# Sixteen attention heads on one core: the order of the steps inside a head

## The chip, the cores and the metric

The kernel is one program on 1 core of one Trainium2 chip. Time is device microseconds of one execution, the median of several runs. The profile is one execution taken by the hardware profiler; its span runs from the first to the last instruction of the program.

## What is computed

One inference step of a two-layer encoder trunk for a prompt (one sequence of 512 frames) and a sample group (8 sequences of 16 new frames, each with 512 cached frames). Layer 0 is a recurrent layer. The residual stream after it gives one shared K and V, and layer 1 is stick-breaking attention with 16 heads of 128 features. The change lies in layer 1 alone; cut to it:

```python
def sb_block(q, q_pos, k, v):
    z = jnp.einsum('bqhd,bshd->bhqs', q, k).astype(jnp.float32) * (HEAD_DIM ** -0.5)
    mask = jnp.arange(k.shape[1])[None, :] < q_pos[:, None]
    log_keep = jnp.where(mask, jax.nn.log_sigmoid(-z), 0.0)
    log_after = lax.cumsum(log_keep, axis=3, reverse=True) - log_keep
    attn = jnp.where(mask, jnp.exp(jax.nn.log_sigmoid(z) + log_after), 0.0)
    o = jnp.einsum('bhqs,bshd->bqhd', attn, v.astype(jnp.float32))

def stick_breaking_mixer(hn, k_all, v_all, w_in, w_out):
    q, zg = jnp.split(hn @ w_in, 2, axis=-1)
    o = stick_breaking(q.reshape(B, T, N_HEADS, HEAD_DIM), k_all, v_all)
    return (o.reshape(B, T, D_ATT) * jax.nn.silu(zg)) @ w_out
```

For each head there are a score matrix, an elementwise function with a running sum from the right, and a sum of value rows weighted by the result. The prompt's queries see the prompt's own keys; the sample's 16 queries of each sequence see its 512 cached keys and its 16 new ones.

## The kernel before

The heads run one after the other (`heads`, L1847). While the attention of head h runs, the query and gate projection of head h+1 is computed beside it, in slices: `query` (L1506) is a generator, and each `next` of it (a step "q") records 12 to 36 matmuls of 128x128 weights against 320 tokens, into the tiles `psh`. A head has 180 of these. In the last head, "q" advances the output projection instead (tiles `acc`, weights `w_out_b`). The float32 operands are split into a high and a low part on ScalarE and VectorE (L1367/L1368 for the weights), and each product takes three matmuls (L108 to L110).

The steps of a head are written as a string of letters, one for the usual head (`ORDER`, L1845) and one for the last (`LAST`, L1844):

- P, `prompt_scores` (L1796): scores of four query rows of blocks, 12 matmuls of 128 weight columns into `z3`, `z2` and `z1`, and 8 matmuls of 32 weight columns for the sample's new keys into the rest of `z1` (L1809). Each goes through `sticks` (L1628): ScalarE abs, exp, ln (L1637 to L1639), VectorE max, scan, subtract (L1642, L1645, L1648), ScalarE exp (L1649), a mask on GpSimd (L1653).
- S0, S1, `sample_scores(g)` (L1723): four matmuls (L1727) of 32 weight columns each against 512 cached keys, one for each of four sequences, into four partition groups of `zc`; then `sticks`. S0 issues the load of the second half's cached keys `ck`.
- V0, V1, `prompt_turn` (L1813): the prompt's attention is transposed on TensorE (`pa`, L1713), copied to `ath` by ScalarE (L1719), and its remainder to `atl` by VectorE (L1720).
- T0, T1, `sample_turn(g)` (L1746): issues the loads of the cached values `cv`, transposes the sample's attention (`pas`, four, and `pan`, one), copied out to `at` and `an`.
- O, `prompt_out` (L1821): 12 matmuls into `po`.
- M0, M1, `sample_out(g)` (L1759): the sum over the values, all with 32 weight columns: four matmuls over the 16 new rows (L1763, operands `an` and `vn`) and 16 over cached rows (L1768, `at` and `cv`), into `pos`; copied out to `ob` by ScalarE (L1771). M0 issues the load of the second half's new values `vn`.
- C0, C1, `sample_close(g)` (L1773): `ob` transposed (`pot`, L1775), multiplied with the gate (L1778); in C1 the head's result is also split into `oh` and a remainder (L1790, L1791) and written to memory by two DMAs of GpSimd's queue (L1793, to `odh` and `odl`).
- L, U, N load the next head's keys, values and first cached keys on SyncE's queue; K and W split them. The raw keys `kr` use the same buffer as `oh`, so L's load waits for the write of `oh`.

An instruction that takes float32 operands as they are (L1727, L1763, L1768, L1809) goes through the array twice and stands twice in the trace: four instructions are eight records.

`pa`, `pas`, `pan`, `po`, `pos` and `pot` take turns in one ring of two PSUM banks (`bank`, L75). `ob`, `at`, `an`, `vn`, `ath`, `atl` and `oh` have one buffer each, `cv` and `ck` two, that is one half's worth. The tile framework's scheduler makes the order on each engine: it follows the written order, puts what can go now ahead of what it takes to be still waiting, and moves up what stands under a high priority (the weight splits, the copies of `psh`).

In the words below a *narrow* matmul is one of 32 weight columns (L1809, L1727, L1763, L1768), and a *narrow block* is a run of them with no other matmul between.

Of the kernel before, what the change touches and what calls it, by code (L numbers as in the profile page):

```python
# [19 lines left out]
P = 128  # L20
# [25 lines left out]
X12, X22, X11, S1, S2, S3, S4 = range(7)  # L46
# [4 lines left out]
class Trunk:  # L51
# [709 lines left out]
    S0 = 3 + TP  # L761
# [926 lines left out]
    def attention(self, h, ap, qkv, zs):  # L1688

        nc, I, O = self.nc, self.I, self.O  # L1690
# [43 lines left out]
        def new_values(g):  # L1734
            t = ap.tile([TS, 4, P], F32, tag="vn", name="vn", bufs=1)
            dma = (nc.gpsimd if g else nc.sync).dma_start
            rows = O["v"][TP + 64 * g : TP + 64 * g + 64, P * h : P * h + P]
            dma(t, rows.rearrange("(b t) d -> t b d", t=TS))
            return t
# [89 lines left out]
        o = zs  # L1829
        if h == NHEAD - 1:  # L1830
            o = self.outs.tile([P, 2, 3 * HALF], F32R, tag="ks1", name="o", bufs=1)[:, 0, :T].bitcast(F32)
        st = {"vn": new_values(0)}
        steps = {"P": prompt_scores, "O": prompt_out}
        for g in range(2):
            steps[f"V{g}"] = lambda g=g: prompt_turn(g)
            steps[f"T{g}"] = lambda g=g: sample_turn(g)
# [4 lines left out]


    STAY = (NHEAD - 2,)
    LAST = "P S0 q q q S1 V0 q V1 q Z T0 M0 O q C0 q T1 q M1 q C1 q"  # L1844
    ORDER = "P q q S0 L q q V0 V1 S1 T0 O U q M0 q T1 N K q C0 M1 W q C1"  # L1845

    def heads(self, count=NHEAD):  # L1847
        with self.pool("att") as ap:
            self.attention_consts(ap)
            self.qraw, self.qready = [None] * 4, {"wh": [], "wl": []}  # L1850
            for i in (0, 1, 3, 2):
                self.query_load(0, i)
            self.qplan = {"wh": self.product_plan(), "wl": self.plain_plan()}
            out = self.attention_begin()
            self.first_query(ap)
            keys, values = self.keys_load(0, ap), self.values_load(0, ap)
            self.ck = self.cached_keys(0, 0, ap)
            k, v = self.keys_split(ap, keys), self.values_split(ap, values)
            for h in range(count):
                qh, ql, qs, zs = self.q  # L1860
                steps = self.attention(h, ap, (qh, ql, qs, *k, *v), zs)
                more = h + 1 < count
                qn = self.query(h + 1, ap) if more else out
                for step in (self.ORDER if more else self.LAST).split():
                    if step == "q":
                        next(qn, 0)
                    elif step == "Z":
                        for j in range(2):
                            self.silu(ap, zs, j)
                    elif step in steps:  # L1870
                        steps[step]()
                    elif more and step == "L":
                        keys = self.keys_load(h + 1, ap)
                    elif more and step == "U":
                        values = self.values_load(h + 1, ap)
                    elif more and step == "N":
                        self.ck = self.cached_keys(h + 1, 0, ap)
                    elif more and step == "K":
                        k = self.keys_split(ap, keys)
                    elif more:  # L1880
                        v = self.values_split(ap, values)
        return out


# [111 lines left out]
def lay_out(r):  # L1996

    heads = lambda v, b: v.reshape(b, -1, NHEAD, P)
    y, k, v = r["y"], r["kT"].T, r["v"]
    state = r["state"].transpose(2, 1, 0).reshape(36, DR)  # L2000
    out = [y[:TP].reshape(1, TP, D), y[TP:].reshape(NB, TS, D), heads(k[:TP], 1), heads(v[:TP], 1), heads(k[TP:], NB),
           heads(v[TP:], NB), state[0:1].reshape(1, 1, DR), state[1:9].reshape(1, NB, DR),
           state[9:12].reshape(1, 1, 3, DR), state[12:].reshape(1, NB, 3, DR)]
    return tuple(np.ascontiguousarray(v) for v in out)
# [14 lines left out]
```

## Time and profile before

| | us |
|---|---|
| runs, median of 3 (lowest to highest) | 2859.81 (2859.26 to 2860.37) |
| span of the profiled execution | 2852.1 |
| what lies around the span | 7.7 |
| TensorE matmul busy in the span | 2785.0 (98%) |
| VectorE, ScalarE, GpSimd busy | 2034.8, 1666.2, 439.1 |
| the new keys' scores (L1809), of head 0 and of head 15, start at | 2020.9 and 2604.7 |

The profile gives the span alone of its execution; the runs' times are of other executions, and 7.7 us is the median less the span. The heads follow one another at 39 to 40 us, head 0 in less. In the views, a row of the timeline has the start, the duration, the engine and line, the operation, the tiles it writes and reads, its shape and how often it stands in a row, with the idle time before it and its releaser in brackets. Matmul ends are modelled: the steps from one start to the next tell how fast TensorE goes, and a matmul's duration is longer than its step.

### The profile page before, as it was taken

The numbers are of one execution on the slowest core, as the hardware profiler recorded it, in microseconds if no ns is written. First come the engines' busy times: TensorE is split into PE (matmuls) and PEld (weight loads), VectorE is DVE, ScalarE is ACT, GpSimd is POOL, SyncE is SP. The second block draws the span as 40 slices with busy tenths as digits, with TensorE's granted clock in tenths as the row PEclk, the third lists the DMA queues.
The fourth block names the chain that finished last, engine by engine and source line by source line (L and its number), as shares of the span: only waits on it lengthen the run. The fifth ranks groups of instructions, "written<-read, shape, count | busy, mean of one in ns | idle before, by whom it ended". The sixth has DMA issues, their size and how long they took to land.

```text
span 2852.1 us, 48054 instructions
## 1 busy us (share of the span) xinstructions
PE 2785.0 (98%) x18340; PEld 2459.3 (86%) x18340; DVE 2034.8 (71%) x3344; ACT 1666.2 (58%) x2846; POOL 439.1 (15%) x732
## 2 busy tenths in 40 slices
PE   6999999999999999999999999999999999999998
PEld 4799999999999987777787899867888889887887
DVE  7678777777777766766866866667877877776335
ACT  5576556655665556665655555553666766666223
POOL 0012212221222111112220000122101111111000
PEclk9999999999999999999999999999999999999999
DMA  9966766676766666676776233575466666668636
GB/s 339 331 145 157 166 161 153 158 164 160 161 149 164 141 228 209 206 251 190 238 255 218 92 117 109 183 267 192 145 205 189 194 197 191 199 199 287 188 111 229
DMA packets 249094, 544.49 MB, mean 191 GB/s; under 512 B 23496, under 2 KB 108616, under 8 KB 247712
## 3 DMA queue, kind: packets, MB, share of 16 engines
q1 hardware_dynamic: 201616, 377.05, 41.2%
q0 software_dynamic: 47248, 164.38, 23.2%
q8 instruction: 144, 2.36, 0.3%
q14 instruction: 86, 0.70, 0.1%
HBM read 499.97 MB, written 41.37 MB: 190 GB/s over the span
## 4 chain that ended last, share of the span: by engine, by line
PE 80%; DVE 4%; ACT 4%; DMA 3%; issue 2%; POOL 0%; SPq 0%; DVEq 0%; POOLq 0%; ACTq 0%
PE acc L108 7%; PE acc L110 7%; PE acc L109 7%; PE pa L108 4%; PE pa L110 4%; PE pa L109 4%; PE psh L108 3%; PE psh L110 3%; PE psh L109 3%; PE pc L110 3%; PE pc L109 3%; PE pc L108 3%; PE acck L108 3%; PE acck L109 2%; PE acck L110 2%
## 5 line engine op out<-in xcount | busy, mean ns | idle before, releaser
L108 PE MATMUL acc<-wh,yh 128*128 128x512 f32 x940 | 371.0, 395 | 0.5 <-ACT wh L93 0.4
L110 PE MATMUL acc<-wh,yl 128*128 128x512 f32 x940 | 365.5, 390 | 1.3 <-DVE yl L962 1.3
L109 PE MATMUL acc<-wl,yh 128*128 128x512 f32 x940 | 366.4, 390 | 0.1
L94 DVE TENSOR_TENSOR wl<-wr,wh 128x1024 fp32r<-128x1024 f32 x151 | 186.5, 1238 | 217.0 <-ACT wh L93 216.6
L93 ACT ACTIVATE wh<-wr 128x1024 fp32r<-128x1024 f32 x151 | 159.6, 1057 | 267.7 <-PE acc L110 220.7
L108 PEld LDWEIGHTS acc<-wh,yh 128*128 128x128 f32 x940 | 176.7, 188 | 54.0 <-issue 15.7
L110 PEld LDWEIGHTS acc<-wh,yl 128*128 128x128 f32 x940 | 176.3, 188 | 38.8 <-DVE yl L962 1.7
L109 PEld LDWEIGHTS acc<-wl,yh 128*128 128x128 f32 x940 | 176.5, 188 | 36.3 <-DVE wl L94 0.7
L193 DVE TENSOR_TENSOR wa<-wa 128x1024 f32<-128x1024 f32 (+1 forms) x160 | 191.5, 1247 | 11.8 <-ACT wa L192 11.2
L110 PE MATMUL pa<-xs,wl 128*128 128x320 f32 x630 | 194.8, 309 | 0.5 <-DVE wl L94 0.5
L108 PE MATMUL pa<-xs,wh 128*128 128x320 f32 x630 | 194.7, 309 | 0.0
L109 PE MATMUL pa<-xs,wh 128*128 128x320 f32 x630 | 194.7, 309 | 0.0
L93 ACT ACTIVATE wh<-sum 128x896 fp32r<-128x896 f32 x102 | 96.9, 950 | 143.0 <-PE pa L109 46.5
L192 ACT ACTIVATE wa<-wa 128x1024 bf16<-128x1024 f32 x160 | 159.3, 1046 | 25.5 <-DVE wa L193 12.0
L546 POOL DMA_DIRECT2D sum<-w_in_a_dram x90 | 79.1, 882 | 490.5 <-DVE wl L94 208.8
L108 PE MATMUL psh<-nh,wl 128*128 128x320 f32 x480 | 150.8, 314 | 2.1 <-DVE z L1535 2.1
L110 PE MATMUL psh<-nh,wl 128*128 128x320 f32 x480 | 150.1, 313 | 0.0
L109 PE MATMUL psh<-nl,wl 128*128 128x320 f32 x480 | 149.4, 311 | 0.0
L93 ACT ACTIVATE wh<-rv 128x256 fp32r<-128x256 f32 (+1 forms) x108 | 51.8, 480 | 145.8 <-PE pa L109 95.2
L108 PE MATMUL acck<-wh,nh 128*128 128x512 f32 x320 | 127.8, 401 | 5.7 <-DVE keep L1263 3.5
L110 PE MATMUL pc<-xs,wl 128*128 128x320 f32 x420 | 129.9, 309 | 0.7 <-DVE wl L94 0.7
L108 PE MATMUL pc<-xs,wh 128*128 128x320 f32 x420 | 130.0, 310 | 0.0
(489 smaller groups left out, 8595.9 us busy)
## 6 DMA issues: line engine op xcount, KB each, us to landing
wa<-w_ada_dram POOLq DMA_DIRECT2D x120, 512.0 KB, 5.2
wr<-w_out_a_dram SPq DMA_DIRECT2D x96, 512.0 KB, 4.5
sum<-w_in_a_dram POOLq DMA_DIRECT2D x90, 448.0 KB, 5.7
wa<-w_ada_dram SPq DMA_DIRECT2D x72, 512.0 KB, 6.4
wr<-w_in_b_dram SPq DMA_DIRECT2D x64, 512.0 KB, 4.3
ck<-cache_k_dram SPq DMA_DIRECT2D x64, 512.0 KB, 5.2
cv<-cache_v_dram SPq DMA_DIRECT2D x64, 512.0 KB, 5.7
wr<-w_out_b_dram SPq DMA_DIRECT2D x55, 512.0 KB, 4.2
```

The source lines that it names most:

```text
L93: self.split_at = nc.scalar.activation(hi[:, :n], raw, AF.Copy).ins
L94: nc.vector.tensor_tensor(lo[:, :n], raw, hi[:, :n].bitcast(F32), ALU.subtract)
L108: mm(out, sh, mh, start=start, stop=False, **kw)
L109: mm(out, sh, ml, start=False, stop=False, **kw)
L110: return mm(out, sl, mh, start=False, stop=stop, **kw)
L192: nc.scalar.activation(parts[i], raw, AF.Copy)
L193: nc.vector.tensor_tensor(parts[2] if i else raw, raw, parts[i], ALU.subtract)
L546: self.nc.gpsimd.dma_start(self.big[tag], self.quarter(w, i), accum_op=ALU.add)
```

## The change

The steps of a head are put in another order. M1 and C1 of a head leave the end of its string: they are kept in `before` and run inside the next head as "m1" and "c1", m1 right behind that head's scores P, c1 one query slice later. The first load of new values `vn`, which had been issued when a head's steps were made, becomes a step X behind m1, since m1 still reads the single buffer. S1 moves from behind V1 to just ahead of M0, V0 and V1 get a query slice between them, O goes behind M0, and T1 stands at the end of the head with one query slice behind it.

```diff
-        st = {"vn": new_values(0)}
-        steps = {"P": prompt_scores, "O": prompt_out}
+        st = {}
+        steps = {"P": prompt_scores, "O": prompt_out, "X": lambda: st.update(vn=new_values(0))}
...
-    LAST = "P S0 q q q S1 V0 q V1 q Z T0 M0 O q C0 q T1 q M1 q C1 q"
-    ORDER = "P q q S0 L q q V0 V1 S1 T0 O U q M0 q T1 N K q C0 M1 W q C1"
+    LAST = "P m1 X S0 q c1 q q S1 V0 q V1 q Z T0 M0 O q C0 q T1 q M1 q C1 q"
+    ORDER = "P m1 X q c1 q S0 L q V0 q V1 T0 q S1 M0 N O U q C0 K q W T1 q"
...
+            before = {}
             for h in range(count):
...
                     elif step in steps:
                         steps[step]()
+                    elif step in ("m1", "c1"):
+                        before.get(step.upper(), lambda: None)()
...
+                before = steps
```

No instruction is added or removed: TensorE has 17,013 matmuls before and after. What moves is where they stand. On TensorE, at the start of a usual head, the scores of the new keys (`z` from `kn`) stood alone between the prompt's scores and the query's matmuls:

```order
L1704 MATMUL z_25274<-kh,ql 128x256
L1809 MATMUL z_25274<-kn,qs 32x16 x8
L108 MATMUL psh<-nh,wh 128x320
L109 MATMUL psh<-nl,wh 128x320
L110 MATMUL psh<-nh,wh 128x320
```

and M1 stood some 12 query matmuls before the head's end. Now, at the same place of the same head, still on TensorE:

```order
L1704 MATMUL z_25241<-kh,ql 128x256
L1809 MATMUL z_25241<-kn,qs 32x16 x8
L1763 MATMUL pos<-vn,an 32x128 x4
L1768 MATMUL pos<-cv,at 32x128 x16
L108 MATMUL psh<-nh,wh 128x320
L109 MATMUL psh<-nl,wh 128x320
```

The sum over the values of the head before has joined the block of the new keys' scores: two narrow blocks have become one. In the middle of a head, on TensorE, the transposes of T0 (`pas`, `pan`) were followed by O before M0, with S1 earlier by itself between transposes:

```order
L1751 MATMUL pas<-ident,e 128x128 x4
L108 MATMUL psh<-nh,wl 128x320
L109 MATMUL psh<-nl,wl 128x320
L110 MATMUL psh<-nh,wl 128x320
L108 MATMUL psh<-nh,wl 128x320
L1755 MATMUL pan<-ident,e 16x128
L109 MATMUL psh<-nl,wl 128x320
L108 MATMUL po<-ath,vh 128x512
```

and now, at that place:

```order
L1751 MATMUL pas<-ident,e 128x128 x4
L1755 MATMUL pan<-ident,e 16x128
L109 MATMUL psh<-ks_20011,wh 128x320
L110 MATMUL psh<-ks_20011,wh 128x320
L1727 MATMUL zc<-ck,qs 32x512 x4
L1763 MATMUL pos<-vn,an 32x128 x4
L1768 MATMUL pos<-cv,at 32x128 x16
L108 MATMUL po<-ath,vh 128x512
```

S1 and M0 have become one block, and O stands behind it. Counted over the heads, TensorE had 83 narrow blocks and has 55, 28 fewer: heads 1 to 13 lose two each, head 0's M1 loses two and head 14's one, and one is added in head 14, where the scheduler cut S1 in two (one matmul, then `pas` and `pan`, then three). The places of the other steps in a usual head are, in query matmuls: before, 60 ahead of S0, 48 to V0, S1 at once, 5 to V1 and 5 within it, 5 to T0; now 27 ahead of C1's `pot`, 33 to S0, 24 to V0, 24 to V1, 10 to T0.

On ScalarE the copy to `ob` that `pot` waits for stood ahead of the next head's `sticks` (`z_25744` is that head's first score matrix):

```order
L1448 ACTIVATE qs<-qr 128x128
L1771 ACTIVATE ob<-pos 128x128
L1367 ACTIVATE wh<-wr 128x512
L1457 ACTIVATE ez<-z 128x320
L1790 ACTIVATE oh<-z 128x640
L1458 ACTIVATE ez<-ez 128x320
L1637 ACTIVATE e<-z_25744 128x512
```

and now it stands inside them, behind fifteen instructions from that head's first score matrix on, of which these are the last eleven:

```order
L1639 ACTIVATE e<-e 128x512
L1637 ACTIVATE e<-z_25724 128x512
L1461 ACTIVATE ez<-ez 128x320
L1638 ACTIVATE e<-e 128x512
L1637 ACTIVATE e<-z_25742 128x256
L1639 ACTIVATE e<-e 128x512
L1638 ACTIVATE e<-e 128x256
L1530 ACTIVATE qr<-psh 128x320
L1367 ACTIVATE wh<-wr 128x512
L1649 ACTIVATE e<-e 128x512
L1639 ACTIVATE e<-e 128x256
L1771 ACTIVATE ob<-pos 128x128
```

C1's writes (`odh`, `odl`) and the load of `kr` behind them come later in the next head for the same reason; on SyncE's queue `kr` now stands behind the second half's `ck` and ahead of three loads of query weights.

## The prediction

> **What bounds the kernel now.** I read the busy times first, then the stretches by window, the waits of TensorE, and last its timeline through one head. The page's line of busy times says who is scarce:
>
> ```profile
> PE 2785.0 (98%) x18340; PEld 2459.3 (86%) x18340; DVE 2034.8 (71%) x3344; ACT 1666.2 (58%) x2846; POOL 439.1 (15%) x732
> ```
>
> TensorE is. The table by windows (stretch, its length, busy time of each engine in the order of its heading, then granted clock, DMA share and GB/s) for head 10, a usual one, and for most of head 15, the last:
>
> ```profile
> 2409.57:2448.59 39.02, 38.89 (x339) 34.83 (x338) 30.82 (x59) 26.84 (x61) 4.82 (x10) 1.00 0.63 196
> 2604.71:2640.00 35.29, 29.06 (x181) 20.89 (x181) 22.56 (x39) 20.82 (x43) 4.55 (x7) 0.90 1.00 348
> ```
>
> In a usual head TensorE works 38.89 of 39.02 us, so an order of steps can gain only in how fast its matmuls follow one another. The last head is another case: 6 us idle, DMA full. The waits of TensorE over all heads (total, times, longest) have two large entries:
>
> ```profile
> PE pos L1768 <- DMA cv<-cache_v_dram: 5.2, 2, 4.0
> PE pa L1713 <- DVE atl L1720: 3.6, 5, 0.9
> ```
>
> The first is head 15's, the second is the second turn V1 waiting for a PSUM bank of V0. The rest has to be read from starts in the timeline, here round S0 and S1 of head 10:
>
> ```profile
> 2417.70 0.31 PE L110 MATMUL psh<-ks,wh 128*128 128x320 f32 x1
> ...
> 2418.58 0.30 PE L110 MATMUL psh<-ks,wh 128*128 128x320 f32 x1
> 2418.81 1.06 PE L1727 MATMUL zc<-ck,qs 128*32 128x512 f32 x8
> ...
> 2427.80 1.07 PE L1727 MATMUL zc<-ck,qs 128*32 128x512 f32 x8
> 2428.79 0.41 PE L108 MATMUL psh<-ks,wh 128*128 128x320 f32 x1
> 2429.04 0.30 PE L109 MATMUL psh<-ks,wh 128*128 128x320 f32 x1
> ```
>
> From 2417.70 to 2418.58 are six steps: a query matmul follows the last after 0.147 us. Into the narrow block the step is 0.23 (0.08 too much), and the first query matmul behind one takes 0.25 (0.10 too much). The same places further on show three more losses:
>
> ```profile
> 2430.48 0.38 PE L1713 MATMUL pa<-ident,e 128*128 128x128 f32 x2
> ...
> 2432.32 0.30 PE L108 MATMUL psh<-nh,wl 128*128 128x320 f32 x1
> 2432.75 0.27 PE L1755 MATMUL pan<-ident,e 128*16 128x128 f32 x1
> 2432.78 0.39 PE L109 MATMUL psh<-nl,wl 128*128 128x320 f32 x1
> 2433.14 0.50 PE L108 MATMUL po<-ath,vh 128*128 128x512 f32 x1
> 2433.47 0.40 PE L109 MATMUL po<-atl,vh 128*128 128x512 f32 x1
> 2433.71 0.39 PE L110 MATMUL po<-ath,vl 128*128 128x512 f32 x1
> ...
> 2435.19 0.42 PE L1763 MATMUL pos<-vn,an 16*32 16x128 f32 x8
> 2435.54 1.08 PE L1768 MATMUL pos<-cv,at 128*32 128x128 f32 x32
> 2436.55 0.41 PE L110 MATMUL psh<-nh,wl 128*128 128x320 f32 x1
> ```
>
> `pan` starts 0.43 us after the matmul before it, 0.28 over the step: it waits for its bank. `po` starts after 0.36 and its second matmul after 0.33, where the third takes 0.24: 0.21 lost, by the ring the wait for the bank of `pas`. And inside M0, from the 16-row matmuls to the 128-row ones, two passes take 0.35 us, while the eight passes behind them take 1.01 with their exit, 0.126 each at most: this joint costs 0.10.
>
> **The change part by part.** *Narrow blocks.* 28 blocks fewer. What goes with each is an entry (0.08) and an exit's slow first matmul (0.10); what comes is a joint within a block. The trace has a joint where the rows stay at 128, the new keys' scores and S0 in head 15:
>
> ```profile
> 2604.72 0.32 PE L1809 MATMUL z<-kn,qs 128*32 128x16 f32 x16
> 2604.87 1.04 PE L1727 MATMUL zc<-ck,qs 128*32 128x512 f32 x8
> ```
>
> Four passes of the first and the joint fit into 0.15 us, so that joint is nearly free. The new joints go from 128 rows to the 16 rows of L1763, the reverse of the one that cost 0.10. Bounds for one block: 0.28 gained if the joint is free and the emptying of the array at the old exit (as much as that 0.10) falls away too; 0.08 if the joint costs 0.10 and the exit held no emptying. I take 0.18, the exit's emptying for the joint's, since the joint changes rows as the measured one does: 28 x 0.18 = 5.0 us (2.2 to 7.8).
>
> The Trainium skill, "TensorEngine Tiling", Key Properties, says that changing the tiling mode, not just the tile, drains TensorE; the entry of 0.23 for 0.147 and the joint of 0.10 agree. By it the new joints still drain and the term is 5.0; without it 7.8.
>
> *pan and po.* O now stands behind a whole narrow block, more than 2 us after `pas`, and its 0.21 goes. `pan` comes ten query matmuls and four `pas` after the last `pa`, 10 x 0.147 + 0.08 + 4 x 0.11 = 2.0 us, where it was free 2.16 us after it (2430.48 and 0.11 to 2432.75). If the copies take as long, 0.16 stays; but S1's first VectorE step no longer stands between them, so up to all 0.28 can go. I take 0.15. In the 13 heads of this order 13 x 0.36 = 4.7 us (2.7 to 6.4).
>
> *V0 and V1 apart.* 24 query matmuls (3.5 us) instead of 5 (0.7 us) stand between; the longest wait was 0.9. Idle time counts from the modelled end, so each wait lost 0.16 more: 3.6 + 5 x 0.16 = 4.4 us in all. I take 3.0, as what delayed VectorE in four or five heads may turn up elsewhere (0 to 4.4).
>
> *C1 in the next head.* This adds a wait. `pot` needs `ob`, and the copy to `ob` stands on ScalarE behind fifteen instructions of the next head's first `sticks`. Rows of TensorE and of ScalarE at the start of head 11, and one copy to `ob`:
>
> ```profile
> 2447.07 0.39 PE L1704 MATMUL z<-kh,ql 128*128 128x512 f32 x1
> 2448.59 0.32 PE L1809 MATMUL z<-kn,qs 128*32 128x16 f32 x16
> ```
>
> ```profile
> 2444.85 0.28 ACT L1771 ACTIVATE ob<-pos 128x128 f32<-128x128 f32 x1 [0.49 <-PE pos L1768]
> ...
> 2448.28 0.45 ACT L1458 ACTIVATE ez<-ez 128x320 f32<-128x320 f32 x1
> 2448.64 0.57 ACT L1637 ACTIVATE e<-z 128x512 f32<-128x512 f32 x1
> ...
> 2452.72 0.38 ACT L1637 ACTIVATE e<-z 128x256 f32<-128x256 f32 x1
> 2452.98 0.44 ACT L1530 ACTIVATE qr<-psh 128x320 f32<-128x320 f32 x1
> 2453.30 0.65 ACT L1367 ACTIVATE wh<-wr 128x512 fp32r<-128x512 f32 x1
> 2453.82 0.64 ACT L1639 ACTIVATE e<-e 128x512 f32<-128x512 f32 x1
> 2454.73 0.63 ACT L1649 ACTIVATE e<-e 128x512 f32<-128x512 f32 x1 [0.27 <-DVE e L1648]
> 2455.27 0.40 ACT L1638 ACTIVATE e<-e 128x256 f32<-128x256 f32 x1
> ```
>
> From 2448.64 to 2455.27 ScalarE ran fourteen instructions in 6.63 us, 0.27 of it waiting. The fifteen ahead of `ob` are these without one copy of `psh` (0.32) and one weight split (0.52), and with one step of the gate (0.36) and two of 256 columns (0.26 each): 6.63 - 0.27 - 0.84 + 0.88 = 6.40. They can begin when the first scores are done, 2447.46, 1.13 us ahead of the L1809 row. So `ob` is done 1.13 less than 6.40 + 0.28 after that row, at 5.55, or 5.82 with the wait. TensorE comes to `pot` after 0.15 + 0.35 + 1.01 for the block and 0.25 + 26 x 0.147 for 27 query matmuls, at 5.58. The wait is 0 to 0.24; I take 0.2, since `pan` and `po`, also put at their earliest moment, came out late: 14 x 0.2 = 2.8 us lost. If all fifteen took the mean of 0.47 us it would be 0.94, 13 us. Behind `pot` stand all of TensorE's query matmuls, so it loses the whole wait.
>
> C1's VectorE and ScalarE work only moves from ahead of the first `sticks` to within them; the cover is that V0's transposes come 15 us into the head. Its writes come later, and `kr` waits for them (size, median us from issue to landing):
>
> ```profile
> odh<-oh POOLq DMA_DIRECT2D x14, 320.0 KB, 4.1
> kr<-out_kT_dram SPq DMA_DIRECT2D x14, 256.0 KB, 2.6
> ...
> wr<-w_in_b_dram SPq DMA_DIRECT2D x51, 512.0 KB, 4.3
> ```
>
> With `oh` about 11 us into the head, `kr` lands at about 18 (11 + 4.1 + 2.6), where ScalarE's split of it stands right behind V0's copies at about 17. ScalarE may stand 1 us, with 24 query matmuls (3.5 us) ahead of the next transposes: nothing, but every us beyond that cover would count. On SyncE's queue `ck` now goes ahead of `kr`, and three loads of query weights wait behind it. They go out from about 15.5 us, where `kr` is released (11 + 4.1 and its issue), and the first lands at about 20, when ScalarE, done with V1's copies, comes to split it; behind that split stands the copy `at` for M0, 2 us later. That is a cover of about 1 us, and a late load beyond it delays M0 by as much; I cost it at nothing. X's load has 20 us, `cv` for M1 gains time (TensorE runs 24 query matmuls and more between): nothing.
>
> *Head 14 and the last head.* Cut in two, S1 takes a second pair of passes, 0.9 us of the 0.99 from 2427.80 to 2428.79. The last head's first `cv` stands on SyncE's queue behind 19 loads of 320 KB after `ck`, before behind 20: at 348 GB/s 0.9 us less (0 to all 5.2 us).
>
> The sum: -5.0 - 4.7 - 3.0 + 2.8 + 0.9 - 0.9 = -9.9 us. On the profiled span of 2852.1 that is 2842.2, and with the 7.7 us that the median of 2859.81 has over it, 2849.9. Head 0, where half the steps differ, I can't cost: 1 us to either side.
>
> **The rivals.** *`pot` in every head (slower).* ScalarE runs in order, and `ob` sits in the middle of a chain that hands back and forth with VectorE. Each us loses 14. The gain is gone when `ob` is 0.7 us later than I take, and from 1.1 us (done 6.9 us into the head) the kernel is slower by more than 0.2%; at 1.5 us later, a wait of 1.7, 2849.9 + 21 = 2871. For it: every step at its earliest moment waited. Against: even the plain mean gives 6.5. Chance 0.06.
>
> *The joints eat the blocks (no change).* Blocks bring 2.2, `po` alone goes (2.7), V1's wait moves to `pan` (1.0 left): -2.2 - 2.7 - 1.0 + 2.8 + 0.9 = -2.2, 2857.6. For it: 0.10 at the only joint that changes rows. Chance 0.16.
>
> *The last head's wait goes (faster still).* These rows show it, and the slower passes behind:
>
> ```profile
> 2630.73 0.64 PE L1768 MATMUL pos<-cv,at 128*32 128x128 f32 x4 [4.04 <-DMA cv<-cache_v_dram]
> 2632.50 1.92 PE L1768 MATMUL pos<-cv,at 128*32 128x128 f32 x28 [1.12 <-DMA cv<-cache_v_dram]
> ```
>
> 28 records take 1.92 us where 32 took 1.08, and the stretch's clock is 0.90. With half the 5.2 us gone and the clock full (0.10 of 35.29 us), 6 us more: 2844. Against it: the loads run at 348 GB/s and start at S0 as before. The Trainium skill, "TensorE: Matmul & The Clock Gate", Part 1, says an idle window of about 3.4 us halves the clock; the 4.04 us here and the rows agree, so a wait cut below that would bring the clock too. Chance 0.08.
>
> **How the numbers follow.** The forecast has 0.70. Range: all terms at their good ends together would give 18.6 us less, 2841.2, which is unlikely, so 2842 is the low end; the no-change rival is taken in up to 2857, and the slower one is left out. About 0.2% (5.7 us) is what a measurement of this kernel can tell from no change: faster is below 2854.1, the forecast and the last rival, 0.78; the same 0.16; slower 0.06.
>
> **What would show it.** Usual heads of about 38.3 us where they had 39.02; joints L1809 to L1763 and L1727 to L1763 without a slow step; `po` at 0.24 from its first matmul on; no wait of `pa` for `atl`. It is wrong if `pot` waits more than 0.5 us, if ScalarE's split of `kr` holds up V1, or if the heads stay at 39 us.

## The result, and the profile after

The changed kernel takes 2924.05 us (median of 4 runs, 2920.27 to 2929.82), the kernel before, run beside it, 2859.53: 1.023 times as long, interval 1.0215 to 1.0244. The forecast of 2849.9 was on the wrong side. The profiled execution has a span of 2923.1 us, 71.0 more than before.

First the busy times of the changed kernel:

```profile
PE 2808.2 (96%) x18340; PEld 2477.5 (85%) x18340; DVE 2034.5 (70%) x3344; ACT 1662.8 (57%) x2846; POOL 445.6 (15%) x732
```

The same number of matmuls makes TensorE busy for 23.2 us more than before (2785.0). Then TensorE's waits over the whole span, those that bear on the heads (total, times, longest):

```profile
PE psh L108 <- DVE z L1535: 50.7, 15, 5.1
...
PE pos L1768 <- DMA cv<-cache_v_dram: 4.1, 2, 2.7
...
PE pa L1713 <- DVE atl L1720: 0.6, 1, 0.6
```

The first is new: the query's matmuls wait for VectorE's L1535, 15 times. One wait of 2.1 us was there before, in head 0; what is new is 48.6 us in 14 heads. With the 23.2 us of busy time that is 71.8, the whole loss and a little more. V1's wait for `atl` is nearly gone, as forecast. A third entry, small here, is new as well: the next head's first scores wait for their query `qh`.

```profile
PE z L1702 <- ACT qh L1446: 2.5, 6, 0.5
```

The wait in head 10, on TensorE, with the seven transposes of V0 ahead of it:

```profile
2470.49 0.93 PE L1713 MATMUL pa<-ident,e 128*128 128x128 f32 x7
2474.85 0.41 PE L108 MATMUL psh<-nh,wl 128*128 128x320 f32 x1 [3.44 <-DVE z L1535]
2475.10 0.31 PE L109 MATMUL psh<-nl,wl 128*128 128x320 f32 x1
```

and on VectorE at the same time:

```profile
2469.62 0.68 DVE L1368 TENSOR_TENSOR wh<-wr,wh 128x512 fp32r<-128x512 f32 x1
2474.31 0.49 DVE L1535 TENSOR_TENSOR z<-psh,qr 128x320 f32<-128x320 f32 x1 [4.00 <-DMA odl<-z]
```

VectorE stood 4.00 us for a transfer, the write `odl<-z`. L1535 takes a query slice out of PSUM and writes it to the gate tile `z` of the head to come. `z` has two buffers, and a head's result replaces its gate in place. While head 10 runs, one buffer holds its own gate, and the other, which L1535 is to fill for head 11, holds head 9's result. Head 9's C1 now runs inside head 10, and its remainder has to land in memory before L1535 may write. Until L1535 has run, the PSUM bank isn't free, and the matmuls behind V0 stand.

How far this was from harmless shows in the rows of both kernels. Before, in GpSimd's and VectorE's rows of head 12:

```profile
2488.77 0.55 POOL L1793 DMA_DIRECT2D odl<-z  x1 [0.57 <-DVE z L1791]
```

```profile
2499.85 0.49 DVE L1535 TENSOR_TENSOR z<-psh,qr 128x320 f32<-128x320 f32 x1 [0.16 <-PE psh L110]
```

and after, in head 10, with who waited for the 14 writes, and the median from issue to landing of these writes, before and after:

```profile
2467.68 0.55 POOL L1793 DMA_DIRECT2D odl<-z  x1 [0.29 <-DVE z L1791]
```

```profile
who waited for it (us, times):
  DVE z L1535: 55.4, 14
```

```profile
odl<-z POOLq DMA_DIRECT2D x14, 320.0 KB, 4.0
```

```profile
odl<-z POOLq DMA_DIRECT2D x14, 320.0 KB, 6.4
```

Before, nobody waited for it. L1535 came 11.08 us after the issue (2499.85 less 2488.77), so with the median landing of 4.0 us some 7.1 us were in hand. After, VectorE reached L1535 at 2474.31 less 4.00, 2.63 us after the issue, and was let go 6.63 us after it. Most of the 4.00 us is the longer landing: had the write landed in 4.0 us, 1.4 us of waiting would have been left. The write is issued 12.8 us into head 10 (2467.68 less 2454.89), where it stood 1.2 us into head 12 (which starts at about 2487.6, by the start of head 11 at 2448.59 and its length): it moved 11.6 us, L1535 only 3.

The busy time belongs to it. The table by windows for heads 10 and 11 (columns as in the prediction), and the wait of head 11:

```profile
2454.89:2497.11 42.22, 38.74 (x339) 34.77 (x339) 30.53 (x59) 26.61 (x61) 5.59 (x10) 1.00 0.58 181
2497.11:2542.19 45.08, 40.65 (x339) 36.16 (x338) 30.91 (x59) 26.51 (x61) 5.15 (x10) 0.96 0.55 170
```

```profile
2517.52 0.63 PE L108 MATMUL psh<-nh,wl 128*128 128x320 f32 x1 [3.91 <-DVE z L1535]
2517.95 0.47 PE L109 MATMUL psh<-nl,wl 128*128 128x320 f32 x1
```

Behind this wait the query matmuls follow at 0.27 us instead of 0.147, eleven of them, and the granted clock of the head is 0.96; by the same table it is 0.50 from 2517.52 to 2520.72. Head 10 waited 3.44 us and went on at 0.147, with a clock of 1.00. By the starts of all 14 waits, twelve were followed by such a stretch, mostly of twelve steps. So a wait cost its own length, and mostly 12 x 0.12 = 1.4 us more.

Head 10 also shows what the rest of the change did, since it has only the wait in it. The step from the last of the seven `pa` to the next matmul is 4.36 - 0.65 = 3.71, where 0.03 is usual. Without it the head takes 42.22 - 3.68 = 38.54 us, 0.48 less than the 39.02 before. The forecast was 38.3, 0.72 less; but 0.21 of that was V1's wait, which head 10 did not have before, so 0.51 could show.

The other heads are longer than this one would suggest. From the first row L1809 of head 1 to that of head 15 the kernel takes 617.2 us (2057.49 to 2674.68) where it took 549.1 (2055.66 to 2604.71), 68.1 more. By the starts of all matmuls between, the steps with the wait for L1535 make 52 us and the slow stretches 19, together 71, so the rest of the change gained about 3 us there. Against it stands the wait for `qh`: the steps into the first scores `z` and those between their matmuls are about 6 us longer than before. Without it the rest would have gained some 9 us by this estimate, near the 9.0 that the sum has for these heads (its 9.9 without the last head).

### The profile page after: what moved, and what is told of

Same layout as the page of the kernel before. It is cut to its first block, busy times and chain, and to the rows that moved or that the text cites. A ratio compares the mean times of both kernels' runs of the same rounds, so it can differ in the third digit from the quotient of the medians.

```text
span 2923.1 us, 48125 instructions
## 1 busy us (share of the span) xinstructions
PE 2808.2 (96%) x18340; PEld 2477.5 (85%) x18340; DVE 2034.5 (70%) x3344; ACT 1662.8 (57%) x2846; POOL 445.6 (15%) x732
## 4 chain that ended last, share of the span: by engine, by line
PE 71%; DVE 7%; DMA 7%; ACT 5%; issue 3%; POOL 0%; DVEq 0%; POOLq 0%; ACTq 0%
PE acc L108 7%; PE acc L110 7%; PE acc L109 7%; PE pa L108 4%; PE pa L110 4%; PE pa L109 4%; DMA odl<-z 3%; PE pc L110 3%; PE pc L108 3%; PE pc L109 3%; DMA vr<-out_v_dram 3%; PE acck L108 2%; PE acck L109 2%; PE acck L110 2%; PE psa L230 2%
## 5 line engine op out<-in xcount | busy, mean ns | idle before, releaser
L108 PE MATMUL psh<-nh,wl 128*128 128x320 f32 x480 | 162.1, 338 | 50.7 <-DVE z L1535 50.7
L109 PE MATMUL psh<-nl,wl 128*128 128x320 f32 x480 | 157.4, 328 | 0.0
L110 PE MATMUL psh<-nh,wl 128*128 128x320 f32 x480 | 157.2, 327 | 0.0
L108 PEld LDWEIGHTS psh<-nh,wl 128*128 128x128 f32 x480 | 99.2, 207 | 56.8 <-DVE z L1535 54.9
L1653 POOL TENSOR_TENSOR e<-e,mask 128x128 f32<-128x128 f32 (+1 forms) x96 | 56.4, 594 | 522.6 <-ACT e L1649 362.9
```

Source lines behind the costliest of these rows:

```text
L108: mm(out, sh, mh, start=start, stop=False, **kw)
L109: mm(out, sh, ml, start=False, stop=False, **kw)
L110: return mm(out, sl, mh, start=False, stop=stop, **kw)
L1653: nc.gpsimd.tensor_tensor(v, v, m, ALU.mult)
```

## The experiments

All times against the kernel before, measured on the same chip beside them.

| run | us | ratio and interval |
|---|---|---|
| own_tile | 2883.45 | 1.0088 (1.0071 to 1.0105) |
| only_c1 | 2927.36 | 1.0241 (1.0226 to 1.0257) |
| c1_stays | 2882.72 | 1.0083 (1.0068 to 1.0098) |
| two_pieces | 2922.99 | 1.0224 (1.0209 to 1.0240) |
| both_free | 2908.14 | 1.0173 (1.0153 to 1.0193) |
| v_and_o | 2859.02 | 1.0001 (0.9990 to 1.0012) |
| ck_later | 2917.62 | 1.0206 (1.0192 to 1.0220) |
| close_first | 2873.83 | 1.0054 (1.0040 to 1.0068) |
| close_first_t0 | 2866.88 | 1.0028 (1.0017 to 1.0038) |
| own_first_t0 | 2866.28 | 1.0031 (1.0019 to 1.0043) |
| close_first_s1 | 2867.97 | 1.0034 (1.0021 to 1.0047) |
| stays_whole | 2875.55 | 1.0060 (1.0043 to 1.0077) |
| v0_later | 2896.71 | 1.0133 (1.0115 to 1.0152) |
| stays_whole_2 | 2875.52 | 1.0060 (1.0046 to 1.0074) |

Theory 1 is the held buffer of `z`. The rivals are that VectorE comes late by its own queue, and that the joints cost the time.

**The remainder in a tile of its own.**

```diff
-                V.tensor_tensor(o, o, oh.bitcast(F32), ALU.subtract)
-                for part, x in zip(self.od, (o, oh.bitcast(F32))):
-                    nc.gpsimd.dma_start(part[P * h : P * h + P, :], x)
+                r4 = ap.tile([P, 4, P], F32, tag="at", name="r4", bufs=1).rearrange("p a n -> p (a n)")
+                r1 = ap.tile([P, P], F32, tag="ob", name="r1", bufs=1)
+                V.tensor_tensor(r4, o[:, :TP], oh[:, :TP].bitcast(F32), ALU.subtract)
...
+                nc.gpsimd.dma_start(self.od[0][rows, :TP], r4)
+                nc.gpsimd.dma_start(self.od[0][rows, TP:], r1)
...
```

> The changed kernel, with the remainder of each head's result (what goes to `odl`) in two tiles that are free at that time (the buffers of `at` and `ob`) instead of in the tile `z`; the write of it becomes two DMAs. Theory 1, the write `odl<-z` holds the buffer of `z` into which the next query is subtracted (L1535): the 50.7 us of TensorE's waits for L1535 fall to about 2 (what before has, once), VectorE's 55.4 us for the DMA `odl<-z` are gone, the clock in the heads is back at 1.00, the heads take 38 to 39 us: 2845 to 2857. Rival 2, VectorE reaches L1535 late by its place in the queue, behind the first `sticks` and C1, and the DMA is only the last of several: the wait stays at 2 us or more a head, 2895 to 2925. Rival 3, the joints inside narrow blocks and `pot` cost the time and the wait is their follower: heads stay over 42 us, over 2900.

It took 2883.45 us, a miss: 2845 to 2857 was expected. TensorE's waits and busy time:

```profile
PE pas L1751 <- DVE atl L1720: 22.9, 14, 2.8
...
PE psh L108 <- DVE z L1535: 2.1, 1, 2.1
```

```profile
PE 2784.8 (97%) x18340; PEld 2459.6 (86%) x18340; DVE 2039.9 (71%) x3358; ACT 1663.6 (58%) x2846; POOL 452.7 (16%) x746
```

The wait for L1535 is back at the one of before, and the busy time too. That settles theory 1 against both rivals: only the remainder's tiles and its write were changed, and C1's work and the joints stood where they had. But some 25 us of loss stay, and a wait is new, T0's `pas` for V1's remainders. Its chain in head 10, on TensorE, VectorE and ScalarE:

```profile
2440.91 0.66 PE L1751 MATMUL pas<-ident,e 128*128 128x128 f32 x4 [1.30 <-DVE atl L1720]
```

```profile
2439.36 0.69 DVE L1317 TENSOR_TENSOR kl<-kr,kh 128x512 fp32r<-128x512 f32 x1 [1.44 <-ACT kh L1315]
2439.96 0.68 DVE L1368 TENSOR_TENSOR wl<-wr,wl 128x512 fp32r<-128x512 f32 x1
2440.57 0.62 DVE L1720 TENSOR_TENSOR atl<-pa,ath 128x128 fp32r<-128x128 f32 x2
```

```profile
2438.69 0.63 ACT L1315 ACTIVATE kh<-kr 128x512 fp32r<-128x512 f32 x1 [1.51 <-DMA kr<-out_kT_dram]
```

This is the other write: `kr` may be loaded only when `odh` has left `oh`'s buffer. ScalarE waits for it 23.2 us in 14 heads, VectorE 22.4 behind ScalarE, and V1's remainders queue behind VectorE's split. In the changed kernel ScalarE waited for `kr` once, for 0.4 us: the longer wait at L1535 had hidden this one.

**M1 and C1 alone, and the rest alone.**

```diff
-    ORDER = "P m1 X q c1 q S0 L q V0 q V1 T0 q S1 M0 N O U q C0 K q W T1 q"
+    ORDER = "P m1 X q c1 q S0 L q q V0 V1 S1 T0 O U q M0 q T1 N K q C0 W q"
```

> Of the change only the move of M1 and C1 (and of the first load of `vn`) into the next head; S1, O, T1 and the distance of V0 and V1 as before. Theory 1: the wait for L1535 appears whole, 3 to 5 us in each of 14 heads, and with it the low clock behind it; against the kernel before 45 to 70 us slower: 2905 to 2930. Rival 2 the same sign, less: the second sum alone makes VectorE late, 2865 to 2900. Rival 3, the time is lost at the block of S1 and M0: within 10 us of before.

2927.36 us, as theory 1 had it: 56.5 us at L1535 in 15 waits, and 2807.1 us busy. The move of M1 and C1, alone, loses as much as the whole change.

```diff
...
-    ORDER = "P m1 X q c1 q S0 L q V0 q V1 T0 q S1 M0 N O U q C0 K q W T1 q"
+    ORDER = "X P q q S0 L q V0 q V1 T0 q S1 M0 N O U q C0 K T1 q W M1 C1 q"
```

> The other half of the change alone: S1 in one block with M0, O behind it, V0 and V1 a query slice apart, T1 towards the end, but M1 and C1 at the end of their own head. Theory 1: no wait for L1535, faster than before by half of the blocks' 5.0 us (2.5), the 4.7 us of `pan` and `po` and up to 3.0 of V1: 2849 to 2855; it may lose 1 to 2 us a head if M1 waits for the copy `at` or for `cv`, with T1 so near. Rival 3 (joints cost): 2860 or more, without any new wait.

2882.72 us, slower than before where 2849 to 2855 was expected. L1535 waits once, as before, but the half didn't come out as written. TensorE in head 11:

```profile
2488.60 1.04 PE L1727 MATMUL zc<-ck,qs 128*32 128x512 f32 x2
2489.58 0.66 PE L1751 MATMUL pas<-ident,e 128*128 128x128 f32 x4
...
2490.38 1.06 PE L1727 MATMUL zc<-ck,qs 128*32 128x512 f32 x6
```

The scheduler put T0's transposes between the first of S1's matmuls and the other three. Four of them side by side take 0.98 us; so cut, they take that twice. 0.98 us a head is 14 us, and V1's transposes waited 9.0 us for `atl`, where before they waited 3.6. The run tells nothing against the joints, and nothing for the gain.

**The same write in two pieces.**

```diff
...
+                for c in (slice(0, HALF), slice(HALF, T)):
+                    V.tensor_tensor(o[:, c], o[:, c], oh[:, c].bitcast(F32), ALU.subtract)
+                    nc.gpsimd.dma_start(self.od[0][P * h : P * h + P, c], o[:, c])
...
```

> The changed kernel, with the remainder computed and written in two pieces, the 320 columns first that L1535 writes over, both still in `z`, and ahead of `odh`. Theory 1: L1535 waits for the first piece only, which has 160 KB instead of 320 and is issued about 1 us sooner; the wait a head falls from 3.4 us to 0.5 to 2.5, and with every wait under 3 us the clock stays higher: 2865 to 2905. Rival 2: the wait stays as it is, 2915 to 2930.

2922.99 us: a miss. L1535 still waits 52.2 us. The median from issue to landing is 6.2 us for pieces of 160 KB, where one of 320 KB took 6.4: half the size bought next to nothing, with `ck` and `odh` under way at the same time.

**The load of `ck` out of the way.** A step Y, behind V0, takes the load of the second `ck` from S0.

```diff
...
-    ORDER = "P m1 X q c1 q S0 L q V0 q V1 T0 q S1 M0 N O U q C0 K q W T1 q"
+    ORDER = "P m1 X q c1 q S0 L q V0 Y q V1 T0 q S1 M0 N O U q C0 K q W T1 q"
```

> The changed kernel, with the load of the second half's cached keys `ck` written behind V0 instead of in S0; the scheduler brings half of it forward, so one of its two transfers of 512 KB still runs beside the writes of C1. If these transfers share what the DMA moves (1.6 MB in 7.6 us in the changed kernel), `odl` lands 1.2 to 2.4 us sooner, VectorE's and TensorE's wait at L1535 falls from 3.4 to 1 to 2.2 us a head, and with no wait over 3.4 us the clock is 1.00 in the heads: 2883 to 2900. Rival, the landing time of a write has its own length and does not depend on the loads: the wait stays, 2918 to 2930.

The median landing of `odl` fell from 6.4 to 4.9 us, and TensorE's wait fell to the upper end of what was expected:

```profile
PE psh L108 <- DVE z L1535: 31.9, 15, 3.3
...
PE pas L1751 <- DVE atl L1720: 11.1, 9, 2.9
```

2.1 us a head instead of 3.5. So the writes do share what the loads use. The time, 2917.62, missed the expectation: `pas` waits took over 11.1 us, S1 was cut in two here as well, and the clock did not come back as a whole. Two heads of this run, at the same place:

```profile
2379.28 0.63 PE L108 MATMUL psh<-nh,wl 128*128 128x320 f32 x1 [3.28 <-DVE z L1535]
2379.72 0.47 PE L109 MATMUL psh<-nl,wl 128*128 128x320 f32 x1
...
2423.62 0.41 PE L108 MATMUL psh<-nh,wl 128*128 128x320 f32 x1 [1.72 <-DVE z L1535]
2423.87 0.31 PE L109 MATMUL psh<-nl,wl 128*128 128x320 f32 x1
```

After 3.28 us of waiting the next step is 0.44 and those behind it 0.27. After 1.72 it is 0.25, and those behind it are 0.15.

**C1 ahead of the `sticks`.** The copy to `ob` in M1 and all that follows `pot` in C1 get the priority of the weight splits.

```diff
-            A.activation(ob, po[:, 0:P], AF.Copy)
+            with self.tc.high_priority(200 * g):
+                A.activation(ob, po[:, 0:P], AF.Copy)
...
```

> The changed kernel, with the copy to `ob` in M1 and what follows `pot` in C1 under the high priority that the weight splits have: on ScalarE `ob` stands eight instructions sooner and `oh` two. Theory 1: the writes go out 0.8 to 1.5 us sooner, the wait at L1535 falls by as much, to 2 to 2.6 us a head, below the 3.4 us of idle time behind which the lower clock showed, so that clock comes back as well (up to 23 us of TensorE's busy time): 2885 to 2905. If the clock does not depend on the length of the wait: 2905 to 2915. Rival 2 (VectorE is late by its own queue): no change, 2918 to 2930. The 0.2 us that `pot` waits for `ob` go in any case.

2873.83 us, faster than the 2885 to 2905 expected by theory 1. All but 2.5 us of the new wait is gone, though the buffers are those of the changed kernel:

```profile
PE psh L108 <- DVE z L1535: 4.6, 5, 2.1
```

The median landing of `odl` is 3.6 us: the writes not only go out sooner, they also go ahead of `ck`. `pot` follows at the usual step. That this repairs it, with no buffer changed, agrees with theory 1; alone it wouldn't exclude a late VectorE, whose order changes here too. What is left over before, some 15 us, looked like S1, cut in two as in c1_stays (14 us by the same 0.98); the runs below bear out half of that.

**`kr` free of the write as well.** Beside own_tile's change:

```diff
...
-        raw = ap.tile([P, T], F32R, tag="oh", name="kr", bufs=1).bitcast(F32)[:, :TP]
+        raw = ap.tile([P, 8, P], F32, tag="cv", name="kr", bufs=2).rearrange("p a n -> p (a n)")[:, :TP]
...
+    ORDER = "P m1 X q c1 q S0 L q V0 K q V1 T0 q S1 M0 N O U q C0 q W T1 q"
```

> The kernel with the remainder in tiles of its own, and besides that the raw keys `kr` loaded into a buffer of `cv` (free from M1's end) instead of `oh`'s, so that this load waits for no write; its split K is written ahead of V1, as `cv` needs the buffer back. Theory 1, second part: there VectorE stood behind the split of `kr` (22.4 us for `kh`, which stood 23.2 us for the transfer), with V1's remainders queued behind it, and TensorE's 22.9 us at `pas` come from that. Expected: those waits under 3 us each, the step into `pas` back at 0.15 instead of 1.6, heads 38.5 to 38.9, 2853 to 2861 in all (the rest over the forecast is in heads 0 and 14 and the last). Rival: VectorE is late there by the sum of its own work, now that C1 and the first `sticks` lie together: `pas` still waits 1 us or more a head, 2870 to 2885. If `cv` comes late for its buffer, TensorE waits for it at M0, which would show as a wait for `cv` in more than the last head.

2908.14 us, a clear miss. No engine waits for `kr` any more, but TensorE and ScalarE do elsewhere:

```profile
PE pas L1751 <- DVE atl L1720: 22.9, 13, 2.6
```

```profile
ACT wh L1364 <- DMA wr<-w_in_b_dram: 33.0, 13, 3.4
```

A third load, the query weights, comes late; in own_tile ScalarE stood for it 15.9 us. It is the load that the prediction named behind `kr`, and here `kr` isn't ahead of it. C1's writes and `ck` are under way beside it, as the issues show, but which of these delays it was not tried. S1 is cut in two here as well. So that `kr` costs own_tile most of its 25 us is read from the chain above, and no run shows it.

**V0, V1 and O in the old order.**

```diff
-    ORDER = "P q q S0 L q q V0 V1 S1 T0 O U q M0 q T1 N K q C0 M1 W q C1"
+    ORDER = "P q q S0 L q V0 q V1 S1 T0 U q M0 O q T1 N K q C0 M1 W q C1"
```

> The kernel before with two of the change's moves and no other: a query slice between V0 and V1 instead of behind T0's place, and O behind M0. By the forecast's terms V1's wait (3.0) and the wait of `po` (0.21 in 13 heads, 2.7) are gone: 2851 to 2857. Rival: the wait goes to the next bank user, T0 or M0, which now follows sooner: 2857 to 2863.

2859.02 us, no difference (0.9990 to 1.0012). The slice between V0 and V1 is taken from ahead of V0, which so comes 24 query matmuls sooner. V1 waits 0.6 us for `atl` instead of 3.6, and these have come:

```profile
PE pos L1763 <- ACT at L1753: 3.6, 6, 1.2
...
PE pa L1713 <- POOL e L1653: 2.3, 3, 1.2
```

M0 now comes too soon for `at`, and V0 for its operand. The rival was right: the waits went to the next user.

**S1 whole again.** Three versions with C1 under priority: T0 ahead of V1; the same with the remainder in its own tiles; S1 ahead of T0 instead. The second has the first one's order.

```diff
...
+    ORDER = "P m1 X q c1 q S0 L q V0 q T0 V1 q S1 M0 N O U q C0 K q W T1 q"
...
+    ORDER = "P m1 X q c1 q S0 L q V0 q V1 S1 T0 q M0 N O U q C0 K q W T1 q"
```

> The changed kernel with C1 under high priority (as in the run close_first) and T0 written ahead of V1 instead of behind it. In close_first the scheduler had put T0's transposes between S1's matmuls, which cost S1 a second pair of passes (0.98 us a head) and the joint to M0 (0.24 by the steps). Now S1 and M0 are one block again. If that is what keeps close_first above the kernel before (15 us over 14 heads, 1.1 a head): heads of 39.2 to 39.5, 2855 to 2862. If the excess is in VectorE's and ScalarE's load at the head's start (V0's waits, 0.5 to 0.8 us a head): 2865 to 2875.

> The same, and the remainder in tiles of its own, so that `z` waits for no write. Against the run before it this takes away what is left of the wait at L1535 (4.6 us in close_first) and adds one DMA a head: 2850 to 2860. If the writes' traffic beside the loads (`ck`, `kr`, the query weights) is what remains, no difference to the run before it, or up to 10 us slower.

> The changed kernel with C1 under high priority, and S1 written right behind V1, ahead of T0, so that S1 is whole but a block by itself, apart from M0. It has one merged block a head (new keys' scores and M1) instead of two, and no second pair of passes. Against close_first 0.98 us a head less at S1, the joint's gain was lost there already: 2858 to 2864 if the split is what costs; 2870 or more if not.

2866.88, 2866.28 and 2867.97 us, all above what was expected if S1 were the whole rest (2855 to 2862, 2850 to 2860, 2858 to 2864): S1 whole is worth 6 to 8 us of the 14, and the tile nothing more, so `z`'s hold is over by then. Over its heads close_first_t0 has these waits:

```profile
PE pa L1713 <- ACT at L1753: 7.5, 9, 1.4
PE pas L1751 <- ACT e L1649: 5.7, 13, 0.7
```

TensorE comes to T0 before its operand is there, and to V1 before T0's copy `at` has freed the bank.

**V0 back at its distance, and the order half alone.** "V0 back" is v0_later, on top of close_first_t0. The first run for the order half, stays_whole, left out the last slice of the next head's query projection (12 of a head's 180 matmuls), so its 2875.55 us are for less work and tell nothing; stays_whole_2 has all of it.

```diff
...
+    ORDER = "P m1 X q c1 q S0 L q q V0 q T0 V1 q S1 M0 N O U C0 q K W T1 q"
...
+    ORDER = "X P q q S0 L q q V0 q T0 V1 q S1 M0 N O U C0 K T1 q q W M1 C1"
```

> M1 and C1 at the end of their own head, as in c1_stays, T0 written ahead of V1, so that S1 and M0 are one block. c1_stays had heads 1.9 us longer than before: S1's second pair of passes 0.9, waits at V1's transposes 1.0 to 1.2. If the split is the cause and V1's waits went with it: heads 38.8 to 39.2, 2850 to 2860; if V1's waits stay, 39.8 to 40.3, 2865 to 2875.

> As close_first_t0, with V0 48 query matmuls behind S0 instead of 24, that is where it stood before the change, and V1, S1 and M0 as much later; S1 and M0 are one block, M1 and C1 in the next head under high priority. close_first_t0 had at V0, T0 and V1 steps of 1.03, 0.96 and more where 0.15 is usual, TensorE waiting for the first `sticks` (V0's and T0's operands): 1.3 us a head. If V0 had come too soon, these go: heads 38.6 to 39.0, 2846 to 2855, the first version under the kernel before. If the head's VectorE and ScalarE work is late by C1 among it, the waits only move to M0 or T1: 2858 to 2870.

> The order half of the change with nothing left out and nothing moved into the next head: S1 and M0 one block, O behind it, V0 at its old place, V1 apart from it, M1 and C1 at the end of their own head. By the forecast's terms: one merged block (0.2 us), `po` 0.21, V1's waits 0.3, a head: heads 38.5 to 38.8, 2850 to 2856. If M1, now 15 query matmuls behind T1, waits for `cv` or `at`, or C0 for `ob`, 0.5 us or more a head: 2857 to 2868.

2896.71 us for v0_later and 2875.52 us for stays_whole_2, both a miss on the slow side. TensorE's waits of the first, and of the second:

```profile
PE z L1702 <- ACT qh L1446: 17.1, 14, 2.0
PE psh L108 <- DVE z L1535: 10.1, 11, 2.2
```

```profile
PE pot L1775 <- ACT ob L1771: 7.5, 13, 0.7
PE pas L1751 <- ACT e L1649: 6.5, 15, 1.6
```

With V0 later, the next head's scores come before `qh` is ready; with M1 and C1 at the end, `pot` comes before `ob`. No version that I ran beats the kernel before. Whether some order would is open.

## Why the prediction was wrong

- **The step that failed** is the part "C1 in the next head", where it says "C1's VectorE and ScalarE work only moves from ahead of the first `sticks` to within them" and follows the later writes to one waiter, `kr`. C1's writes read two buffers, `oh` and `z`. Who writes `z` next, L1535, was not asked. The prediction had the numbers: `oh` about 11 us into the head, and a landing of 4.1 us from there. The rows of before had L1535 11.08 us after the write's issue with some 7.1 us in hand; the write moved 11.6 us into its head against L1535's 3, and then took 6.4 us to land instead of 4.0. Cost: 48.6 us of waiting and, by the lower clock behind it, most of the 23.2 us of busy time.
- **`kr` at nothing** was wrong as well, though it didn't show in the result. Alone (own_tile) it makes ScalarE wait 23.2 us, 1.7 us a head, where I had it stand 1 us at most, with 3.5 us of query matmuls as the cover. The cover followed ScalarE only: VectorE's half of the split waits behind ScalarE's, V1's remainders stand behind that, and TensorE waits 22.9 us for them, 1.6 us a head. The landings of 4.1 and 2.6 us were taken from places where no `ck` was under way; in own_tile they are 4.9 for `odh` and 4.1 for `kr`. A split of `kr` that holds up V1 was named as what would show the forecast wrong.
- **The wait for `qh`** is a second term that the sum did not have: about 6 us, by the steps into and between the scores. Why `qh` comes later was not tried: neither only_c1 nor c1_stays has it among its waits, and in v0_later it is 17.1 us.
- **The blocks** held. The rows of the changed kernel at M0:

```profile
2481.28 1.06 PE L1727 MATMUL zc<-ck,qs 128*32 128x512 f32 x8
2482.27 0.42 PE L1763 MATMUL pos<-vn,an 16*32 16x128 f32 x8
2482.62 1.08 PE L1768 MATMUL pos<-cv,at 128*32 128x128 f32 x32
2483.63 0.50 PE L108 MATMUL po<-ath,vh 128*128 128x512 f32 x1
2483.97 0.39 PE L109 MATMUL po<-atl,vh 128*128 128x512 f32 x1
2484.20 0.39 PE L110 MATMUL po<-ath,vl 128*128 128x512 f32 x1
```

From S1 to L1763 takes 0.99 us, as S1's own exit did before (2427.80 to 2428.79). So the joint costs what the exit had cost, and the entry of 0.08 and the slow first matmul of 0.10 are saved: 0.18 a block, the value taken. The Trainium skill's "TensorEngine Tiling", Key Properties, has a change of the tiling mode drain TensorE; 0.99 for 0.99 agrees. The other joint, from L1809 to L1763, takes 0.25 us (2454.90 to 2455.15), as L1809's exit did before (2448.59 to 2448.84). This is read from the rows; no run changed the blocks alone.
- **`po`**: its second matmul still takes 0.34 (2483.63 to 2483.97), but for another reason: it is now the first matmul behind a narrow block that is slow, a step that before fell on a query matmul behind M0 (2436.55 to 2436.80). In head 0 of before, where `po` came at the usual step, its second matmul took 0.23 (2042.55 to 2042.78). So the sign named for it, 0.24 from the first matmul on, could not show, though the wait itself is gone. `pan` and V1's wait went as forecast, but v_and_o shows that this, by itself, is paid back in the next wait.
- **`pot`**: forecast 0.2 us, and so it is, its step is 0.33 to 0.36 for 0.15 in 13 heads. (The wait of 0.94 that the prediction gives for the plain mean counts 0.27 us of waiting twice; it should be 0.67.) In head 10:

```profile
2460.43 0.31 PE L110 MATMUL psh<-nh,wl 128*128 128x320 f32 x1
2460.78 0.33 PE L1775 MATMUL pot<-ident,ob 128*128 128x128 f32 x1
```

- **The last head** waits 4.1 us for `cv` where it waited 5.2: 1.1 less, forecast 0.9. The agreement may be luck: other runs with the same steps in the last head wait 4.5 (two_pieces, close_first) to 5.2 us (close_first_s1).

So the terms that were summed gave 0.48 of the 0.51 us that could show in the head that can be read clean, and over heads 1 to 14, with the wait for `qh`, about 3 of 9.0 us. A term that was not in the sum was seven times as large as the gain of that clean head. The rivals had the slow side by `pot`; none of them had a write that holds a buffer.

## What to carry to other kernels

When a step moves later, list the buffers that its last instruction, the DMA that writes the result out among them, still reads, and for each the instruction that next writes that buffer; then set the move against the time between landing and that writer in the trace of before. A result that is kept in place of its operand, as `o` in `z`, doubles such waiters. When one hold is lifted, expect the next to show: here a wait of 3.5 us a head had hidden one of 1.6. And take the landing time from a place with the same transfers beside it: 4.0 us had become 6.4.

## What the runs showed of the hardware

A wait of TensorE far shorter than I had thought brings the low clock: in ck_later, at the same place, six waits of 1.71 to 1.79 us were followed by the usual steps, and six of the eight from 1.83 to 3.30 us by a stretch at 0.267 us a step, mostly twelve of them, 3.2 us long. The granted clock is 0.50 in such a stretch (2378.31 to 2385.14) and 1.00 behind the wait of 1.72 us (2423.00 to 2427.00). The length alone does not decide: two waits of 1.87 us in ck_later and 3.44 us in head 10 of the changed kernel went without. The Trainium skill's "TensorE: Matmul & The Clock Gate", Part 1, has the clock halve after an idle window of about 3.4 us, and calls that window free-running. That waits of like length went both ways agrees; but here a wait of 1.83 us, about half such a window, was enough.

A write's time to landing depends on what else is under way: `odl` had a median of 4.0 us before, 6.4 beside two loads of `ck`, 4.9 beside one, 3.6 ahead of them, and beside two 6.2 for half its size.
